# Sixteen feature tiles by seven products, with the weights' block sums made by accumulating transfers

## The chip, the cores and the metric

The kernel runs on one core of a Trainium2 chip. A time is the device's microseconds for one execution. Three runs of the kernel before gave 2389.67, 2389.71 and 2389.91 us, median 2389.71.

## The reference

A decoder trunk of two layers on x of 512 tokens by 1024 features, float32. A layer is a half-step feed-forward, a mixing of three attention branches, and a second half-step feed-forward, each inside RMS norms. The change touches the four feed-forwards alone:

```
D_FF = ((8 * D_MODEL // 3 + 127) // 128) * 128          # 2816 = 22 tiles of 128
def _swiglu(t, w_gate, w_up, w_down):
    return (jax.nn.silu(t @ w_gate) * (t @ w_up)) @ w_down
...
h = h + 0.5 * _rmsnorm(_swiglu(_rmsnorm(h, ffn1_pre_g[l]), ...), ffn1_post_g[l])
```

## The kernel before

**Numbers in two halves.** TensorE multiplies in fp32r. Each operand is split into a high half h (a rounding copy on ScalarE, line 188) and a low half l (source minus h on VectorE, line 189), and a product is three matmuls: h·h, h·l, l·h (`mm3`, lines 214 to 216).

**Weights.** A `Unit` (line 241) is 128x1024 numbers, 512 KB. `fetch` issues its load on SP into one of two "raw" tiles, `load` issues the split into one of four "wh" and one of four "wl" tiles. A `Queue` (line 372) holds the jobs of TensorE in order; when a job starts, the units of the next jobs, four of them, are loaded, so their splits are placed one to two jobs ahead. The order on each engine is fixed when the program is built.

**Feed-forward** (`ffn`, line 642). The 22 feature tiles are made in three ways. Plain jobs (`gates`, `ups`) multiply eight blocks of weights with the tokens for a pair of tiles. Groups of four tiles (`group`, line 766; tiles 2 to 13 in three groups) cut tokens and weights into 2x2 blocks, gate and up side by side, and make the four result blocks with seven products instead of eight (Winograd's form of Strassen's method), tokens on the partitions. The order of the products is `ORDER = (0, 2, 3, 4, 5, 1, 6)`, 24 matmuls of 512 columns each. A group ends with `feature_major` (line 751): 16 transposes and four copies bring its hidden values back to features on the partitions. The first 16 hidden tiles go through the down projection by seven products as well, in two groups of eight tiles (`products`, line 882), the last six plainly (`down`).

**Block sums.** The factors of the seven products are blocks of the weights and sums of them. `BlockUnit` (line 288) loads the blocks from HBM on SP, seven loads for each half of a group, and VectorE makes four sums with `tensor_tensor` on 128x1024 numbers (lines 337, 340, 345, 349) in two kept tiles: kt (tag "v") for gate and up, bt (tag "k") for down. The sums of the tokens (`sums`) and of the hidden values (`first_factor`) are made on VectorE too.

**Order around the change.** In a feed-forward: tile pair 0 (`halved`), pair 14 plainly, groups 2, 6 and 10, then pairs 16, 18 and 20 plainly, their gate and up jobs put between the products of the two down groups. PSUM's eight banks are two tags of four: "mm" for gate and up, "z" for transposes and the down groups. GpSimd (POOL) has little to do: memsets, small copies, two mask selects at the start (lines 144 and 150) and three small loads.

Of the kernel before, what the change touches and what calls it, by code (L numbers as in the profile page):

```python
# [22 lines left out]
def kernel(  # L23
# [84 lines left out]
    def blk(tag, name):  # L108
        return stile([P, 2, S], tag, name)
# [178 lines left out]
    class BlockUnit(Unit):  # L288
# [39 lines left out]
        def load(self):  # L328
# [25 lines left out]
                Q.fetched -= 1  # L354
            Q.fetch_ahead()

    class Keep:


# [274 lines left out]
    W_H, W_U = 4.8, (8.0, 7.0, 7.0, 5.7)  # L634


    TG = (2, 6, 10)

    HR = ("q", "q", "o", "o", "o", "tri", "tri", "rs")
    ORDER = (0, 2, 3, 4, 5, 1, 6)  # L640

    def ffn(l, src, wg, wu, wd, dst, name, spare, aside=None):
# [9 lines left out]
        def hidden(f, pg, pu):  # L652
            s = tmp(f"s{name}_{f}")
            nc.scalar.activation(s[:], pg[:], AF.Silu)
            if f < NC * FC:
                nc.vector.tensor_tensor(pair(f)[:, f % 2], pu[:], s[:], ALU.mult)
                return
            nc.vector.tensor_tensor(s[:], pu[:], s[:], ALU.mult)
            t = blk("q" if f >= 20 else "o", f"hid{name}_{f}")
# [91 lines left out]
        def feature_major(f):  # L751

            for i in range(2):
                u = st.pop(("hid", f, i))
                for b in range(2):
                    f2 = f + 2 * b
                    pt = pbank("z", f"th{name}_{f2}_{i}")
                    for m in range(2):
                        for e in range(2):
                            nc.tensor.transpose(pt[:, (2 * m + e) * P:(2 * m + e + 1) * P],  # L760
                                                u[:, e, (2 * b + m) * P:(2 * b + m + 1) * P], ident[:])
                    yield 0.45
                    out_ = pt[:].rearrange("p (m q) -> p m q", m=2)
                    nc.scalar.copy(pair(f2)[:, :, HALVES[i]], out_)

        def group(f):

            keep = Keep(lambda i, k0: stile([P, 2, S], "v", f"kt{name}_{f}_{i}_{k0}", F32)[:])
            for n in ORDER:
                uns = []  # L770
                for k in range(0, ND // 2, 2):
                    uns.append(BlockUnit(n, wg[l], ND // 2, k, 2, S, keep, f"t{name}_{f}_{n}_{k}", (wg[l], wu[l])))
# [56 lines left out]
        def first_factor(ci, n):  # L829

            nm = f"{name}_{ci}_{n}"
            h, l = (stile([P, FC // 2, S // 2], "v", f"a{x}{nm}")[:] for x in "hl")
            if n == 2:
                st["s", ci] = stile([P, FC // 2, S // 2], "v", f"as{nm}", F32)[:]
            for b in range(2):
                a = lambda i, j: hr[FC // 2 * ci + 2 * j + b][:, :, HALVES[i]]
                two = slice(2 * b, 2 * b + 2)
                s = st["s", ci][:, two] if ("s", ci) in st else None
                if n == 2:
                    nc.vector.tensor_tensor(s, a(1, 0), a(1, 1), ALU.add)  # L840
# [7 lines left out]
                split(h[:, two], l[:, two], from_, scale=-1.0 if n == 6 else None)  # L848
            st["a", ci, n] = h, l


# [30 lines left out]
        def products(ci):  # L882

            def make(i, k0):
                if k0 == 0:
                    st["bt", i] = stile([P, 2, 2, S], "k", f"bt{name}_{i}", F32)
                return st["bt", i][:, k0 // 2]

            keep, w = Keep(make), wd[l, ci * FC * P:(ci + 1) * FC * P]
            for n in ORDER:  # L890
                uns = [BlockUnit(n, w, FC // 2, k, 2, S, keep, f"d{name}_{ci}_{n}_{k}") for k in range(0, FC // 2, 2)]
                yield uns, (lambda n=n, uns=uns: product(ci, n, uns))

        marks, todo = {}, iter(())
# [7 lines left out]
        def some(n):  # L902
            for one in itertools.islice(todo, n):
                Q.add(*one)
# [44 lines left out]
        todo = iter(())  # L949
        pairs = [(wpair(wg[l], ND, f * P, f"g{name}_{f}"), wpair(wu[l], ND, f * P, f"u{name}_{f}")) for f in (16, 18)]  # L950
        Q.add(pairs[0][0], lambda: gates(16, pairs[0][0]))
        behind()
        todo = downs(0)
        Q.add(pairs[0][1], lambda: ups(16, pairs[0][1]))
        some(3)
        Q.add(pairs[1][0], lambda: gates(18, pairs[1][0]))
        some(7)
        Q.add(pairs[1][1], lambda: ups(18, pairs[1][1]))
        todo = downs(1)
        some(3)  # L960
        norm = aside() if aside is not None else None
        xg, xu = wpair(wg[l], ND, 20 * P, f"g{name}_20"), wpair(wu[l], ND, 20 * P, f"u{name}_20")
        Q.add(xg, lambda: gates(20, xg))
        some(4)
        if aside is not None:
            Q.add([], lambda: iter((next(norm),)))
        Q.add(xu, lambda: ups(20, xu))
        if aside is not None:
            Q.add([], lambda: iter((next(norm),)))
        if aside is not None:  # L970
            Q.add([], lambda: norm)
        f0 = NC * FC
        hact = lambda k, c=FULL: tuple(part[:, c] for part in hid[f0 + k])

# [96 lines left out]
    def mem_norm(l, mn):  # L1071
# [1 line left out]
        mn[:] = [stile([P, ND, M], "tri", f"mn{l}_{i}") for i in range(2)]  # L1073
        raws = []
        for t in range(MT):
            raws.append(stile([P, D], "v", f"mraw{l}_{t}", F32))
            nc.sync.dma_start(raws[t][:], mem[0, t * P:(t + 1) * P, :])
        yield 0.0
        for t in range(MT):
# [658 lines left out]
```

## Time and profile before

| | |
|---|---|
| median of 3 runs | 2389.71 us |
| profiled execution | 2390.63 us, its span 2388.9 us |
| granted TensorE clock | 0.999 |
| transfers | 334.00 MB, mean 140 GB/s |
| POOL's own queue (q0) | 96 packets, 0.03 MB |

The names of tiles in the views end with the feed-forward they belong to: a for the first of a layer, c for the second. pta, ptc are PSUM tiles of the gate-up groups, pda, pdc of the down projection, pga and pua of plain gate and up jobs; wh and wl are the halves of weights, tha the transposes of `feature_major`.

### The profile page before, as it was taken

What the parts mean: (1) busy time and instruction counts of PE and PEld (TensorE: products, weight loads), DVE (VectorE), ACT (ScalarE), POOL (GpSimd) and SP (SyncE); (2) the same over time, 40 slices, a digit from 0 to 9 for tenths busy, and PEclk for the clock granted to TensorE, in tenths of its full rate; (3) what the DMA queues carried; (4) which work ended last, traced back from release to release, by engine and by line L of the source; (5) the groups of instructions that cost most, each with busy time, mean ns of one, the idle gap of its engine ahead of it and who ended that gap; (6) DMA issues with size and microseconds to landing.
All of it is one profiled execution on the core that took longest, in us unless ns stands there. A gap on an engine that the chain in (4) does not pass through costs nothing.

```text
span 2388.9 us, 30985 instructions
## 1 busy us (share of the span) xinstructions
PE 2377.2 (100%) x11736; PEld 2010.7 (84%) x11736; DVE 1842.9 (77%) x2535; ACT 1320.8 (55%) x2144; POOL 74.2 (3%) x130
## 2 busy tenths in 40 slices
PE   9999999999999999999999999999999999999998
PEld 8888888888888898888898888888888888988887
DVE  7786887677876687769787878876787766778686
ACT  5655455576655555554545554656675655455543
POOL 0000000001110000000000000000001100000000
PEclk9999999999999999999999999999999999999999
DMA  5554554222223445545545546532232244445453
GB/s 188 165 174 136 202 183 143 71 76 77 88 62 116 158 135 174 169 148 195 184 141 166 178 140 220 174 109 80 63 98 71 71 141 142 159 143 183 141 198 129
DMA packets 233979, 334.00 MB, mean 140 GB/s; under 512 B 10315, under 2 KB 133475, under 8 KB 233829
## 3 DMA queue, kind: packets, MB, share of 16 engines
q1 hardware_dynamic: 233728, 331.98, 42.8%
q8 instruction: 92, 1.51, 0.3%
q14 instruction: 59, 0.48, 0.1%
q0 software_dynamic: 96, 0.03, 0.0%
q10 hardware_dynamic: 4, 0.00, 0.0%
HBM read 319.39 MB, written 12.58 MB: 139 GB/s over the span
## 4 chain that ended last, share of the span: by engine, by line
PE 95%; DVE 3%; ACT 1%; DMA 1%; issue 0%; DVEq 0%; ACTq 0%
PE pg L216 3%; PE pg L214 3%; PE pg L215 3%; PE pta L214 3%; PE ptc L216 3%; PE pta L216 3%; PE ptc L215 3%; PE pta L215 3%; PE ptc L214 3%; PE pda L214 3%; PE pda L215 3%; PE pda L216 3%; PE pdc L216 3%; PE pdc L215 3%; PE pdc L214 3%; PE pb L214 2%
## 5 line engine op out<-in xcount | busy, mean ns | idle before, releaser
L214 PE MATMUL pg<-us_a,wh_wg 128*128 128x512 f32 x384 | 150.6, 392 | 0.0
L216 PE MATMUL pg<-us_a,wl_wg 128*128 128x512 f32 x384 | 149.6, 390 | 0.0
L215 PE MATMUL pg<-us_a,wh_wg 128*128 128x512 f32 x384 | 149.5, 389 | 0.0
L188 ACT CAST wh_tc<-ktc 128x1024 fp32r<-128x1024 f32 x60 | 62.6, 1052 | 83.3 <-DVE ktc L349 32.4
L188 ACT CAST wh_ta<-kta 128x1024 fp32r<-128x1024 f32 x60 | 62.6, 1053 | 80.2 <-DVE kta L349 34.1
L189 DVE TENSOR_TENSOR wl_tc<-ktc,wh_tc 128x1024 fp32r<-128x1024 f32 x60 | 72.8, 1223 | 24.4 <-ACT wh_tc L188 24.2
L189 DVE TENSOR_TENSOR wl_ta<-kta,wh_ta 128x1024 fp32r<-128x1024 f32 x60 | 72.9, 1223 | 23.4 <-ACT wh_ta L188 22.9
L216 PE MATMUL pdc<-wh_dc,alc 128*128 128x512 f32 x224 | 87.3, 390 | 0.3 <-DVE alc L189 0.3
L215 PE MATMUL pdc<-wl_dc,ahc 128*128 128x512 f32 x224 | 87.2, 389 | 0.0
L214 PE MATMUL pdc<-wh_dc,ahc 128*128 128x512 f32 x224 | 87.1, 389 | 0.0
L214 PE MATMUL pda<-wh_da,aha 128*128 128x512 f32 x224 | 87.1, 389 | 0.0
L215 PE MATMUL pda<-wl_da,aha 128*128 128x512 f32 x224 | 87.1, 389 | 0.0
L216 PE MATMUL pda<-wh_da,ala 128*128 128x512 f32 x224 | 87.1, 389 | 0.0
L192 DVE SCALAR_TENSOR_TENSOR wl_wg<-raw_wg,wh_wg 128x1024 fp32r<-128x1024 f32 x48 | 58.8, 1224 | 34.0 <-ACT wh_wg L191 29.5
L216 PEld LDWEIGHTS pg<-us_a,wl_wg 128*128 128x128 f32 x384 | 72.1, 188 | 15.2
L215 PEld LDWEIGHTS pg<-us_a,wh_wg 128*128 128x128 f32 x384 | 72.2, 188 | 14.3
L214 PEld LDWEIGHTS pg<-us_a,wh_wg 128*128 128x128 f32 x384 | 72.1, 188 | 14.3
L214 PE MATMUL pta<-wh_ta,aga 128*128 128x512 f32 x192 | 75.2, 391 | 0.0
L214 PE MATMUL ptc<-wh_tc,agc 128*128 128x512 f32 x192 | 75.0, 391 | 0.0
L216 PE MATMUL pta<-wh_ta,aga 128*128 128x512 f32 x192 | 74.7, 389 | 0.0
L216 PE MATMUL ptc<-wh_tc,agc 128*128 128x512 f32 x192 | 74.7, 389 | 0.0
L215 PE MATMUL ptc<-wl_tc,agc 128*128 128x512 f32 x192 | 74.7, 389 | 0.0
(536 smaller groups left out, 7691.3 us busy)
## 6 DMA issues: line engine op xcount, KB each, us to landing
raw_da<-in_ffn_w_down_dram SPq DMA_DIRECT2D x58, 512.0 KB, 3.6
raw_dc<-in_ffn_w_down_dram SPq DMA_DIRECT2D x58, 512.0 KB, 3.4
raw_ta<-in_ffn_w_gate_dram SPq DMA_DIRECT2D x48, 512.0 KB, 3.7
raw_wg<-in_w_gate_dram SPq DMA_DIRECT2D x48, 512.0 KB, 3.5
raw_tc<-in_ffn_w_gate_dram SPq DMA_DIRECT2D x48, 512.0 KB, 3.6
kta<-in_ffn_w_up_dram SPq DMA_DIRECT2D x24, 512.0 KB, 4.9
raw_wo<-in_w_out_dram SPq DMA_DIRECT2D x24, 512.0 KB, 3.3
ktc<-in_ffn_w_up_dram SPq DMA_DIRECT2D x24, 512.0 KB, 5.7
```

Of the source, the lines that this page charges most:

```text
L188: both = [nc.scalar.copy(h_ap, src)]
L189: make = lambda: nc.vector.tensor_tensor(l_ap, src, h_ap.bitcast(F32), ALU.subtract)
L192: make = lambda: nc.vector.scalar_tensor_tensor(l_ap, src, scale, h_ap.bitcast(F32), ALU.mult, ALU.subtract)
L214: nc.tensor.matmul(pt, lh, rh, start=start, stop=False, skip_group_check=free)
L215: nc.tensor.matmul(pt, lh, rl, start=False, stop=False, skip_group_check=free)
L216: nc.tensor.matmul(pt, ll, rh, start=False, stop=stop, skip_group_check=free)
```

## The change

- The pairs 14 and 16 join as a fourth group (14 to 17), so 16 tiles are made by seven products. Pair 18 takes the place of the early plain pair; only pair 20 stays between the groups, its gate job ahead of the first down group and its up job between the two down groups. Tiles 16 and 17 are split straight from the transposes.
- `SumUnit` replaces `BlockUnit`. VectorE's sums are gone. A tile is negated by ScalarE (`minus`), and a block from HBM, or another tile, is added by a DMA that accumulates, issued by GpSimd (`plus`). Each half of a gate-up group has three kept tiles, six "v" tiles in all, with four accumulating transfers; each half of a down group has two kept tiles with five. Five plain loads are left in each.
- The tiles of mem for `mem_norm` take tag "o" in place of "v", and its parts stand between the products of the second down group.

```
+    class SumUnit(BlockUnit):
+        BLOCKS = ((0, 0), (1, 0), None, None, (1, 1), None, None)
+        def __init__(self, n, src, rows, k0, nk, ncol, keep, name, pair=None, three=True):
+            super().__init__(n, src, rows, k0, nk, ncol, keep, name, pair)
+            self.kept = {2: 0, 3: 2 if three else 1, 5: 1, 6: 0}.get(n)
+            self.three = three
+        def buf(self, i):
+            return self.keep.get(i, self.k0)
+        def plus(self, i, b):
+            if isinstance(b, int):
+                src = self.buf(b)
+            else:
+                r = (b[0] * self.rows + self.k0) * P
+                src, c = (self.src, b[1] * self.ncol) if self.pair is None else (self.pair[b[1]], self.c0)
+                src = src[r:r + self.nk * P, c:c + self.ncol].rearrange("(k p) c -> p k c", p=P)
+            nc.gpsimd.dma_start(self.buf(i), src, accum_op=ALU.add)
+        def minus(self, i, src):
+            nc.scalar.activation(self.buf(i), src, AF.Copy, scale=-1.0)
+        def fetch(self):
...
+            if self.n == 0:
+                self.block(self.buf(1), (0, 1))
+                if self.three:
+                    self.block(self.buf(2), (0, 0))
+        def load(self):
...
+            self.split_from(self.raw[:] if self.kept is None else self.buf(self.kept))
+            if self.n == 0:
+                self.minus(0, self.raw[:])
+                self.plus(0, (0, 1))
+                self.minus(1, self.buf(1))
+                self.plus(1, (1, 1))
+            elif self.n == 2:
+                if self.three:
+                    self.plus(2, 1)
+                else:
+                    self.plus(1, (0, 0))
+            elif self.n == 3:
+                self.minus(0, self.buf(self.kept))
+                self.plus(0, (1, 0))
+                if not self.three:
+                    self.block(self.buf(1), (0, 1))
+            elif self.n == 4 and not self.three:
+                self.minus(1, self.buf(1))
+                self.plus(1, (1, 1))
...
-    HR = ("q", "q", "o", "o", "o", "tri", "tri", "rs")
+    HR = ("q", "q", "o", "o", "o", "o", "o", "tri")
...
-                    nc.scalar.copy(pair(f2)[:, :, HALVES[i]], out_)
+                    if f2 < NC * FC:
+                        nc.scalar.copy(pair(f2)[:, :, HALVES[i]], out_)
+                        continue
+                    if i == 0:
+                        st["hp", f2] = [stile([P, 2, S], "o", f"hid{x}{name}_{f2}") for x in "hl"]
...
+                    split(h[:, :, HALVES[i]], low[:, :, HALVES[i]], out_)
...
-        plain(14, 1, 1)
+        plain(18, 1, 1)
...
-        for g in (6, 10):
+        for g in (6, 10, 14):
...
+        gates_()
         behind()
         todo = downs(0)
...
+        some(7)
+        ups_()
+        todo = downs(1)
+        some(1)
+        norm_()
+        some(3)
+        norm_()
         some(3)
+        norm_(True)
```

More of the change, by code (lines that the diff above doesn't have):

```diff
@@ L847, in first_factor @@
                 from_ = a(*((0, 0), (0, 1), None, None, None, None, (1, 1))[n]) if n in (0, 1, 6) else s
-                split(h[:, two], l[:, two], from_, scale=-1.0 if n == 6 else None)
+                split(h[:, two], l[:, two], from_)
             st["a", ci, n] = h, l
@@ L890, in products @@
             for n in ORDER:
-                uns = [BlockUnit(n, w, FC // 2, k, 2, S, keep, f"d{name}_{ci}_{n}_{k}") for k in range(0, FC // 2, 2)]
+                uns = [SumUnit(n, w, FC // 2, k, 2, S, keep, f"d{name}_{ci}_{n}_{k}", three=False) for k in range(0, FC // 2, 2)]
                 yield uns, (lambda n=n, uns=uns: product(ci, n, uns))
@@ L948, in ffn, with gates_, ups_, norm_ @@
             later[:] = over
-        todo = iter(())
-        pairs = [(wpair(wg[l], ND, f * P, f"g{name}_{f}"), wpair(wu[l], ND, f * P, f"u{name}_{f}")) for f in (16, 18)]
-        Q.add(pairs[0][0], lambda: gates(16, pairs[0][0]))
+        norm = aside() if aside is not None else None
+        xg, xu = wpair(wg[l], ND, 20 * P, f"g{name}_20"), wpair(wu[l], ND, 20 * P, f"u{name}_20")
+        def gates_():
+            Q.add(xg, lambda: gates(20, xg))
+        def ups_():
+            Q.add(xu, lambda: ups(20, xu))
+        def norm_(whole=False):
+            if aside is not None:
+                Q.add([], lambda: norm if whole else iter((next(norm),)))
+        gates_()
         behind()
         todo = downs(0)
-        Q.add(pairs[0][1], lambda: ups(16, pairs[0][1]))
+        some(7)
[3 more added lines that the diff above has]
+        norm_()
         some(3)
[L956 to L959, printed above, removed]
+        norm_()
         some(3)
[L961 to L971, printed above, removed]
+        norm_(True)
         f0 = NC * FC
```

25 lines of the change are left out of this document (21 added, 4 removed).

## The prediction

> **What bounds the kernel now.** I read the page first: its busy shares and the chain that ended last. Then I asked for what TensorE waits for in the whole span.
>
> ```profile
> span 2388.9 us, 30985 instructions
> PE 2377.2 (100%) x11736; PEld 2010.7 (84%) x11736; DVE 1842.9 (77%) x2535; ACT 1320.8 (55%) x2144; POOL 74.2 (3%) x130
> PE 95%; DVE 3%; ACT 1%; DMA 1%; issue 0%; DVEq 0%; ACTq 0%
> PE warm L1608 <- DVE warm L1692: 1.3, 1, 1.3
> PE ptf L1176 <- DVE pf L1247: 0.7, 2, 0.4
> ```
>
> The chain is 95% TensorE, and the waits of TensorE that have a name add up to 4.3 us in seven rows, of which the first two stand here. So nothing but TensorE's own instructions sets the time: an instruction taken off another engine gives nothing back, one taken off TensorE gives its pace, and every new wait of TensorE is paid in full. The pace is not the duration in the groups, since matmuls overlap. It comes from a timeline of TensorE and from the chain in order of time:
>
> ```profile
> 65.72 0.39 PE L214 MATMUL pta<-wh_ta,aga 128*128 128x512 f32 x1
> ...
> 70.93 0.39 PE L216 MATMUL pta<-wh_ta,aga 128*128 128x512 f32 x1
> ```
>
> ```profile
> 109.69 1.75 PE tha L760 x16
> 149.54 1.75 PE tha L760 x16
> ```
>
> The first two rows are matmuls 1 and 24 of one product: 5.21 us for 23 steps, 0.2266 us a matmul of 512 columns. A product (24) takes 5.44 us; a weight unit, half of it, takes u = 2.72 us. Sixteen transposes take 1.75 us. The start to start distance of the two rows, 39.85 us, is a whole group: 7 products (38.1) and one turn (1.75).
>
> **The change, part by part.**
>
> *TensorE.* Four more feature tiles go through seven products in place of eight: 24 fewer matmuls and 16 more transposes per feed-forward, and there are four of these. The instruction orders of the two built programs have it so: 96 fewer 128x512 matmuls, 64 more 128x128 transposes. That is 96 x 0.2266 = 21.8 us less and 4 x 1.75 = 7.0 us more: **-14.8 us**, all on the path.
>
> *VectorE and ScalarE.* 128 sums of 128x1024 leave VectorE, 160 negations of that size come to ScalarE, which is busy 55%. By the reading above both count as nothing, as long as no split comes late. I therefore ask how far ahead the splits run.
>
> ```profile
> L188 ACT CAST wh_da<-bta x40: 1047/1053/1059, 199.2 to 1487.0; 128x1024 fp32r<-128x1024 f32 x40
> L189 DVE TENSOR_TENSOR wl_da<-bta,wh_da x40: 1212/1222/1228, 200.3 to 1488.1; 128x1024 fp32r<-128x1024 f32 x40
> 267.39 1.05 ACT L188 CAST wh_da<-bta 128x1024 fp32r<-128x1024 f32 x1 [1.41 <-PE pda L216]
> 270.11 1.06 ACT L188 CAST wh_ga<-raw_ga 128x1024 fp32r<-128x1024 f32 x1 [1.67 <-PE pda L216]
> 167.18 1.05 ACT L188 CAST wh_ta<-kta 128x1024 fp32r<-128x1024 f32 x1 [3.90 <-DVE kta L349]
> ```
>
> The splits of consecutive units stand 2.72 us apart and wait for TensorE, because there are four buffers of each half: unit i is split when unit i-4 is used up, three units (8.2 us) before it is needed. The split takes 1.05 + 1.22 us, so 5.9 us are in hand. The last row is a split that came 3.9 us late, and TensorE did not feel it.
>
> *The accumulating transfers.* 208 are new: 8 in each gate-up group, 10 in each down group, 512 KB each. They follow a negation on ScalarE and are followed by a split on ScalarE, in ScalarE's fixed order. Let X be the time from the end of the negation to the landing. Nothing in this trace accumulates, so X is bounded by its neighbours: plain transfers, and small ones on the same queue.
>
> ```profile
> raw_wo<-in_w_out_dram SPq DMA_DIRECT2D x24, 512.0 KB, 3.3
> kta<-in_ffn_w_up_dram SPq DMA_DIRECT2D x24, 512.0 KB, 4.9
> bta<-in_ffn_w_down_dram SPq DMA_DIRECT2D x16, 512.0 KB, 5.5
> L123 POOL DMA_DIRECT2D vecs<-in_mem_norm_g_dram x1: 580/580/580, 35.1 to 35.1; - x1
> DMA to landing us min/median/max: 1.8/1.9/2.1
> 100.00:104.00 4.00, 4.00 (x19) 3.33 (x18) 3.96 (x5) 2.01 (x4) 0.00 (x0) 1.00 1.03 369
> 110.00:150.00 40.00, 40.00 (x188) 33.38 (x187) 32.04 (x32) 21.41 (x29) 0.00 (x0) 1.00 0.57 185
> ```
>
> The last two columns of the windows are the share and the GB/s of the 16 transfer engines: full, they move 369 GB/s, so 512 KB (0.524 MB) need 1.4 us of all sixteen; 1.9 us more is what a tiny transfer takes, and the sum, 3.3, is the first row. X cannot be under that 3.3. If the destination must be read too, the work doubles: 1.9 + 2.8 = 4.7. Beside other transfers the plain ones take 1.6 to 2.2 us more (second and third rows); with that X is 6.3 to 6.9. The upper end is three plain passes of 5.5 us one after another, 16.5. I take **X = 7**, nearest to the doubled work in company. Then I look for what each X costs.
>
> 1. *Down products, fourth to fifth factor.* In units from the start of product 0, buffer 1 is free after the split of unit 4 (u + 2.3 = 5.0 us), is loaded again (to 9.5 or so), is negated behind unit 6's split (to 11.1), accumulates, and is split as unit 8, which TensorE needs at 8u = 21.8; less 2.3 for the split, 19.5. So X may be 8.4, and 8.1 for the unit's twin: **8.2**. Beyond it TensorE waits X - 8.2, in 8 places.
> 2. *Gate-up groups.* POOL issues a group's transfers in a fixed order: the sum of buffers 2 and 1 waits there for an earlier landing, and the transfer into buffer 0, which the group's second product needs, is queued behind it. The first negation ends at about 22 us (buffer 1's second half is free after unit 8's split at 5u + 2.3, then 4 us of load and the negation behind unit 10's split), so buffer 0 lands at 22 + 2X + 1 and must land by 16u - 2.3 = 41.2: **X up to 9.1**, beyond it 2(X - 9.1) in 12 places.
> 3. *The start.* In the first feed-forward two mask selects stand on POOL behind an accumulate that waits for another one, and VectorE's copies of the masks stand, in fixed order, ahead of the first weights' low half.
>
> ```profile
> 18.64 2.36 DVE L189 TENSOR_TENSOR wl_ua<-raw_ua,wh_ua 128x1024 fp32r<-128x1024 f32 x2
> 27.80 1.15 POOL L144 TENSOR_SCALAR_AFFINE_SELECT c<-c 128x128 f32<-128x128 f32 x1 [19.73 <-DVE c L143]
> 28.99 0.23 DVE L146 CAST causal<-c 128x128 bf16<-128x128 f32 x1 [0.18 <-POOL c L144]
> 29.27 0.48 DVE L149 MEMSET c<- 128x512 f32 x1
> 31.33 0.43 DVE L152 CAST begins<-c 128x512 bf16<-128x512 f32 x1 [0.50 <-POOL c L150]
> 31.69 1.21 DVE L684 TENSOR_TENSOR ra<-ra,ra 128x1024 f32<-128x1024 f32 x1
> 31.71 0.07 DVE L155 MEMSET c<- 104x8 f32 x1
> 32.82 0.68 DVE L157 TENSOR_SCALAR c<-ident 8x8 f32<-8x8 f32 x4
> 33.53 1.23 DVE L678 TENSOR_TENSOR ra<-us_x 128x1024 f32<-128x1024 f32 x1
> 34.68 0.17 DVE L158 COPY sel<-c 104x8 f32<-104x8 f32 x1
> 34.75 2.35 DVE L189 TENSOR_TENSOR wl_ga<-raw_ga,wh_ga 128x1024 fp32r<-128x1024 f32 x2
> 38.40 0.39 PE L216 MATMUL pga<-us_x,wl_ga 128*128 128x512 f32 x1
> ```
>
>    Buffer 1's load starts when the first low half of the second row's pair (wl_ua) is done, at 19.9; it lands at 24.8 and is negated by 25.9. The first accumulate lands at 25.9 + X = 32.9, POOL issues the next (0.6) and runs the select (1.15): the copy starts at 34.7 and not at 28.99. Behind it stand these steps of VectorE (4.5 us with the copy) and one low half of 1.22 that used to come after wl_ga; then the first half of wl_ga itself (1.22) ends at 41.6 at best, for a matmul that now starts at 38.40: **3.2 us**, once; it grows one for one with X and is gone at X = 3.8.
> 4. *The last turn.* Before, product 0 of the down projection came after an up job of 10.9 us; now it follows the turn of the last group at once, in the same four PSUM banks.
>
> ```profile
> L764 ACT COPY hra<-tha x24: 568/602/628, 111.4 to 1375.9; 128x512 f32<-128x512 f32 x24
> ```
>
>    ScalarE's order puts the split of product 2's second unit (1.05, free only when the gate job ends) and a negation (1.05) ahead of the four copies; the second copied bank needs VectorE's low half as well. From the end of the gate job: 0.6 + 1.05 + 2 x 0.55 + 0.7 = 3.5 us against 1.75 of transposes and 0.68 of matmuls that can go first: **1.05 us, four times, 4.2 us**.
>
> *SP's queue.* It issues 72 fewer loads; the two mem loads now wait for "o" tiles that the first down group has read by then. Nothing; if that group were late, the loads behind them on SP would be as late.
>
> The sum goes against the profiled execution, 2390.6 us (span 2388.9 and 1.7 around it): 2390.6 - 14.8 + 3.2 + 4.2 = 2383.2. The median of the runs is 0.9 lower: **2382.3 us**.
>
> The Trainium skill has a rule against this change. "Collectives: The Full Stack", section "The bandwidth ceiling: the fold count and why AG ≠ RS ≠ AR", says that a reducing transfer runs at half the rate of a copy, since the add needs two source reads, and not because adding is slow. No run here shows it. "DMA: Bandwidth & Descriptors", section "Anatomy of one DMA", gives 2.0 us and 436 GB/s for a transfer of this queue; with two reads X would be 4.4 us by estimate, and the sum 2379.7.
>
> **The rivals.**
>
> - *Late landings* (slower). If issuing such a transfer takes GpSimd several microseconds (the 0.58 above is for eight rows), or company costs more, X passes 8.2. At 8.8 points 1 to 4 eat the whole gain; at 10 the cost is 14 in point 1, 22 in point 2, 6 at the start, 4.5 at the turns: 2421. At 12: about 2490. For it: these chains have no slack to spare. Against it: the estimate from the rows stays under 8.
> - *The transfer engines become the bound* (slower). With doubled work a down group holds 10 x 1.4 + 10 x 2.8 = 42 us of transfers beside 38.1 us of products, a gate-up group 14 + 22.4 = 36.5 beside 39.85. Gate and up jobs between the groups (21.8 us with 5.6 us of transfers) make up for the 4 us. With tripled work it is 56 and 48, which is 18 over (less 8 for those jobs) and 8 over: 8 x 10 + 12 x 8 = 176 us, 2550. This is the rule of the two source reads taken one pass further; with two it does not bind.
> - *The full gain* (faster). If X is under 5 or the start and the turns find cover, 2375 to 2380.
> - *It doesn't do what it says*: the work taken off VectorE is worth nothing here, since VectorE ends no wait of TensorE above 0.7 us. That is in the sum already; only the 14.8 us count.
>
> **How the numbers follow.** My forecast (X from 5.5 to 8.3, 2380 to 2385) has 0.37, the full gain 0.12, X between, where gain and cost cancel, 0.11, late landings 0.32, full transfer engines 0.08. A measurement can tell about 0.2% (4.8 us) from no change, so faster is under 2384.9: 0.48; slower over 2394.5: 0.40; within: 0.12. The range goes down to the full gain less a little, 2374, and up to X = 10.5, 2440, which leaves out the far end of late landings and the full engines. The likeliest case's own range is 2379 to 2386.
>
> **What would show it.** TensorE: 96 and 64 in the counts, groups still 39.85 us apart. The landing of the POOL transfers into kta and bta: 6 to 8 us. In TensorE's waits: wl_ga once, about 3 us; pda for a copy or low half after the turn, about 1 us four times; none for wh_ta or wh_da. I would be wrong if landings were above 8.2 us: then wh_da (fifth factor) and wh_ta (second product) appear among TensorE's waits 8 and 12 times; or if the share of the transfer engines were near 1 through whole groups.

## The result, and the profile after

The changed kernel takes **2567.8 us** (median of 4 runs, 2564.4 to 2570.8) against 2389.7 before: 1.0746 times as long, interval 1.0732 to 1.0759. It is slower by 178 us, where 7 us less was forecast. The profiled execution took 2564.4 us; its span is 2562.7 us, 173.8 longer than before.

The page of the changed kernel, in the order busy time, queues, chain:

```profile
PE 2434.1 (95%) x11704; PEld 2026.9 (79%) x11704; DVE 1695.0 (66%) x2415; ACT 1503.2 (59%) x2358; POOL 313.2 (12%) x338
q0 software_dynamic: 52576, 109.09, 25.1%
PE 54%; DMA 23%; DVE 8%; ACT 7%; issue 7%; POOL 1%; ACTq 0%; POOLq 0%; SPq 0%; DVEq 0%
```

The chain was 95% TensorE; now 23% of it are transfers. TensorE sits idle for 128.6 us (11.7 before), and though it has 14.8 us less to do it is busy for 57 us more. Two losses, then: waits, and slower matmuls. The waits of TensorE (line waited for, us in total, times, longest):

```profile
PE ptc L214 <- ACT cc L810: 23.4, 11, 3.7
PE pta L214 <- ACT ca L810: 22.5, 11, 4.0
PE pda L214 <- ACT hra L836: 8.8, 2, 4.4
PE pda L214 <- ACT aha L188: 7.9, 2, 4.4
...
PE vecs_t L128 <- DMA vecs<-in_b_gate_dram: 4.1, 1, 4.1
PE pda L215 <- DVE wl_da L189: 3.7, 6, 0.8
...
PE pga L216 <- DVE wl_ga L189: 1.0, 1, 1.0
```

The large ones are not for weights. Line 810 is ScalarE's Silu of the seventh product, which empties two PSUM banks (an evacuation); line 836 copies the transposes, which empties four; aha and ahc are factors made of hidden values. Landings of the transfers (the last column, us):

```profile
bta<-in_ffn_w_down_dram POOLq DMA_DIRECT2D x40, 512.0 KB, 8.1
kta<-in_ffn_w_up_dram POOLq DMA_DIRECT2D x32, 512.0 KB, 8.2
```

The turns (the 16 transposes) of the four groups of the first feed-forward, from timelines of TensorE, with the first matmul of the first group and the last down matmul:

```profile
66.08 0.80 PE L214 MATMUL pta<-wh_ta,us_x 128*128 128x512 f32 x1
...
127.76 1.91 PE L831 MATMUL tha<-ident,ca 128*128 128x128 f32 x16
...
175.45 1.91 PE L831 MATMUL tha<-ident,ca 128*128 128x128 f32 x16
...
222.67 1.91 PE L831 MATMUL tha<-ident,ca 128*128 128x128 f32 x16
...
262.51 1.91 PE L831 MATMUL tha<-ident,ca 128*128 128x128 f32 x16
...
409.73 0.39 PE L216 MATMUL pda<-wh_da,hida 128*128 128x512 f32 x1
```

They are 47.69, 47.22 and 39.84 us apart: a group costs nothing extra when no group follows it. Such rows cut every run into stages, summed over the four feed-forwards below: the gate-up stage from the first matmul of the groups to the last turn, the down stage from there to the last down matmul. "Counted" is the kernel before with the 14.8 us off: each gate-up stage 128.6 us plus a group of 39.85, the down stages the rest. The stage columns come from each run's profiled execution, the last column is the run's time.

| kernel | gate-up stages | down stages | whole, us |
|---|---|---|---|
| counted for the new order | 674 | 491 | 2376 |
| the changed kernel | 761 | 585 | 2567.8 |
| VectorE's sums (e1) | 675 | 517 | 2408.0 |
| transfers for gate and up only (e3) | 760 | 516 | 2501.3 |
| transfers for down only (e4) | 687 | 594 | 2491.1 |
| plain transfers (e5) | 676 | 512 | 2401.4 |
| evacuation first (e6) | 738 | 597 | 2553.0 |
| and POOL's order (e12) | 702 | 598 | 2515.9 |

Of e3 to e7, e10 and e12 there is one time each, of the others a median. The changed kernel's profiled execution is 189 us above the count of its own order. Of these, 87 are lost in the gate-up stages, all but some 3 of them in twelve places, three in each feed-forward; 94 are lost in the down stages, 5.9 at the start and 1.7 elsewhere.

**One of the twelve places, on three engines.** TensorE first, at the second product of the second group (start, duration, and in brackets the idle time before it with what ended it):

```profile
117.18 0.50 PE L214 MATMUL pta<-wh_ta,aga 128*128 128x512 f32 x1 [3.96 <-ACT ca L810]
...
120.67 0.80 PE L214 MATMUL pta<-wh_ta,aga 128*128 128x512 f32 x1 [1.95 <-ACT ca L810]
121.26 0.63 PE L215 MATMUL pta<-wl_ta,aga 128*128 128x512 f32 x1
...
125.10 0.51 PE L215 MATMUL pta<-wl_ta,aga 128*128 128x512 f32 x1
```

ScalarE, in its fixed order, shortly before:

```profile
115.59 1.04 ACT L188 CAST wh_ta<-kta 128x1024 fp32r<-128x1024 f32 x1 [6.06 <-DMA kta<-in_ffn_w_up_dram]
116.54 0.59 ACT L810 ACTIVATE ca<-pta 128x512 f32<-128x512 f32 x1
119.07 1.04 ACT L188 CAST wh_ta<-kta 128x1024 fp32r<-128x1024 f32 x1 [1.94 <-DMA kta<-in_ffn_w_up_dram]
120.02 0.59 ACT L810 ACTIVATE ca<-pta 128x512 f32<-128x512 f32 x1
```

Each Silu needs 0.59 us. Its input was ready at about 108, when the last matmul of the seventh product was through, but it stands behind a split that waits for a landing. And GpSimd, which issued those transfers:

```profile
91.96 1.20 POOL L382 DMA_DIRECT2D kta<-in_ffn_w_up_dram  x1 [21.49 <-ACT kta L385]
95.02 1.20 POOL L382 DMA_DIRECT2D kta<-in_ffn_w_up_dram  x1 [1.85 <-ACT kta L385]
99.88 0.90 POOL L382 DMA_DIRECT2D kta<-kta  x1 [3.66 <-DMA kta<-in_ffn_w_up_dram]
105.06 0.86 POOL L382 DMA_DIRECT2D kta<-kta  x1 [4.28 <-DVE wl_ta L189]
105.61 2.79 POOL L382 DMA_DIRECT2D kta<-in_ffn_w_up_dram  x2
```

The first transfer, issued at 91.96, has landed by 99.88. The last two go into buffer 0; they could not be issued before the two sums of tiles, and are used at 115.59 and 119.07, 10 and 12 us later. The transfer engines are full while these wait (the last two columns are their share and GB/s):

```profile
96.00:116.00 20.00, 17.22 (x76) 13.92 (x75) 9.25 (x10) 8.32 (x9) 4.46 (x5) 1.00 1.05 233
```

The second loss is in the granted clock (the column behind POOL's busy time):

```profile
112.00:116.00 4.00, 1.22 (x6) 0.68 (x4) 0.00 (x0) 0.41 (x1) 0.00 (x0) 1.00 1.10 239
116.00:120.00 4.00, 1.27 (x3) 0.48 (x3) 1.23 (x1) 2.06 (x3) 0.00 (x0) 0.81 0.61 132
120.00:124.00 4.00, 3.33 (x8) 2.69 (x9) 2.89 (x3) 4.00 (x7) 2.14 (x2) 0.50 0.08 6
```

After the wait the clock is granted at half, and from 121.26 to 125.10 nine matmuls take 0.427 us each instead of 0.2266: 1.8 us on top of the wait. In the whole timeline 180 steps from one matmul of a product to the next are 0.39 to 0.46 us long, none before; they alone are some 36 us more than at full pace.

### The profile page after: what moved, and what is told of

It reads as the page before. It is cut to its first block, busy times and chain, and to the rows that moved or that the text cites. A ratio compares the mean times of both kernels' runs of the same rounds, so it can differ in the third digit from the quotient of the medians.

```text
span 2562.7 us, 31463 instructions
## 1 busy us (share of the span) xinstructions
PE 2434.1 (95%) x11704; PEld 2026.9 (79%) x11704; DVE 1695.0 (66%) x2415; ACT 1503.2 (59%) x2358; POOL 313.2 (12%) x338
## 3 DMA queue, kind: packets, MB, share of 16 engines
q0 software_dynamic: 52576, 109.09, 25.1%
## 4 chain that ended last, share of the span: by engine, by line
PE 54%; DMA 23%; DVE 8%; ACT 7%; issue 7%; POOL 1%; ACTq 0%; POOLq 0%; SPq 0%; DVEq 0%
DMA ktc<-in_ffn_w_up_dram 7%; DMA kta<-in_ffn_w_up_dram 5%; DMA bta<-in_ffn_w_down_dram 4%; PE pg L216 3%; PE pg L214 3%; PE pg L215 3%; DMA btc<-in_ffn_w_down_dram 3%; DVE wl_tc L189 1%; PE pb L214 1%; PE pb L216 1%; PE pb L215 1%; PE pda L215 1%; PE pda L214 1%; PE pda L216 1%; PE pq L214 1%
## 5 line engine op out<-in xcount | busy, mean ns | idle before, releaser
L189 DVE TENSOR_TENSOR wl_ta<-kta,wh_ta 128x1024 fp32r<-128x1024 f32 x64 | 78.3, 1224 | 109.7 <-ACT wh_ta L188 109.6
L189 DVE TENSOR_TENSOR wl_tc<-ktc,wh_tc 128x1024 fp32r<-128x1024 f32 x64 | 78.3, 1223 | 108.4 <-ACT wh_tc L188 108.4
L214 PE MATMUL pta<-wh_ta,aga 128*128 128x512 f32 x256 | 107.5, 420 | 23.3 <-ACT ca L810 22.5
L214 PE MATMUL ptc<-wh_tc,agc 128*128 128x512 f32 x256 | 106.3, 415 | 23.4 <-ACT cc L810 23.4
L215 PE MATMUL pta<-wl_ta,aga 128*128 128x512 f32 x256 | 105.4, 412 | 1.6 <-DVE wl_ta L189 1.6
L214 PE MATMUL pdc<-wh_dc,ahc 128*128 128x512 f32 x224 | 92.6, 414 | 15.0 <-ACT hrc L836 7.0
L215 PE MATMUL ptc<-wl_tc,agc 128*128 128x512 f32 x256 | 105.1, 411 | 1.3 <-DVE wl_tc L189 1.3
L216 PE MATMUL pta<-wh_ta,aga 128*128 128x512 f32 x256 | 104.6, 408 | 0.0
L216 PE MATMUL ptc<-wh_tc,agc 128*128 128x512 f32 x256 | 104.1, 407 | 0.0
L189 DVE TENSOR_TENSOR wl_tc<-raw_tc,wh_tc 128x1024 fp32r<-128x1024 f32 x48 | 58.4, 1223 | 60.4 <-ACT wh_tc L188 60.4
L189 DVE TENSOR_TENSOR wl_ta<-raw_ta,wh_ta 128x1024 fp32r<-128x1024 f32 x48 | 58.6, 1224 | 58.0 <-ACT wh_ta L188 57.8
L382 POOL DMA_DIRECT2D ktc<-in_ffn_w_up_dram x32 | 40.4, 1299 | 389.2 <-ACT nhb L582 280.9
```

What stands on the lines that cost most here:

```text
L189: make = lambda: nc.vector.tensor_tensor(l_ap, src, h_ap.bitcast(F32), ALU.subtract)
L214: nc.tensor.matmul(pt, lh, rh, start=start, stop=False, skip_group_check=free)
L215: nc.tensor.matmul(pt, lh, rl, start=False, stop=False, skip_group_check=free)
L216: nc.tensor.matmul(pt, ll, rh, start=False, stop=stop, skip_group_check=free)
L382: nc.gpsimd.dma_start(self.buf(i), src, accum_op=ALU.add)
```

## The experiments

The theory after reading the trace: the accumulating transfers land late, and what TensorE then misses is mostly not the weights but work queued behind a waiting split on ScalarE. The rivals: full transfer engines, the new order of the jobs, GpSimd's issue.

**e1, VectorE's sums in the new order.**

```
-uns.append(SumUnit(n, wg[l], ...))    +uns.append(BlockUnit(n, wg[l], ...))
-uns = [SumUnit(n, w, ...)]            +uns = [BlockUnit(n, w, ...)]
-split(h[:, two], l[:, two], from_)    +split(h[:, two], l[:, two], from_, scale=-1.0 if n == 6 else None)
```

> The changed kernel's four groups and order of jobs, with the block sums back on VectorE (no accumulating transfer). Theory (the accumulating transfers and what stands behind them in fixed orders cost everything): the 14.8 us of TensorE come out, less at most the 1 us at each of the four last turns: 2375 to 2380 us. Rival (the new order itself costs: the down groups back to back, the last turn ahead of them): the 96 us that the down stages lost in the changed kernel stay at least in part, 2420 us or more.

Measured 2408.0 us, 1.0073 times before (1.0059 to 1.0086). Both expectations missed, and it is the main surprise: without a single accumulating transfer the sixteen tiles make the kernel slower. The gate-up stages take what was counted to a microsecond; the down stages lose 26 us, and most of the rest is lost right behind them, where TensorE waits for the norm (utc and uta, 4.7 us in all). VectorE's windows in the first down stage (third busy figure), and what TensorE waits for:

```profile
231.00:271.00 40.00, 40.00 (x178) 32.84 (x176) 38.04 (x46) 24.56 (x35) 0.00 (x0) 1.00 0.41 134
271.00:311.00 40.00, 37.22 (x155) 29.53 (x155) 37.73 (x46) 20.40 (x27) 0.00 (x0) 0.96 0.56 193
```

```profile
PE pda L214 <- ACT aha L188: 5.6, 5, 2.2
```

VectorE is busy 95% (88% before, in its windows from 230 to 310, when gate and up jobs stood between these products), and the factors of hidden values come late.

**e2, the transfers in the old order.** SumUnit in the kernel before, nothing else.

> The kernel before, with its three groups and its jobs between the products of the down groups; only the block sums are made by negation and accumulating transfers. Theory (late landings): two places of some 7 us in each of four feed-forwards, 57 us, and some 10 us in the down stages of each, which the gate and up jobs between cover in part: 2470 to 2500 us. Rival (full transfer engines: 40.7 us of their time in a gate-up group of 39.85, but room in the down stages, where 132 us stand against 141): under 2450 us. Rival (the new order of jobs costs): 2390 to 2400 us.

Measured 2483.0 us, 1.0392 (1.0378 to 1.0406), as the theory had it. The gate-up stages lose 63 us, nearly all of it in eight such places. So the transfers cost 92 us without the new order, and the rival of full engines, which had under 2450, is weakened.

**e3 and e4, the transfers in one stage only.** SumUnit kept for gate and up (e3) or for down (e4), BlockUnit in the other.

> The changed kernel, with the sums of the down groups back on VectorE; accumulating transfers in the gate-up groups alone. Theory (each stage pays for its own transfers): 2567.8 less the 96 us that the down stages lost, 2465 to 2480 us, with the three places per feed-forward at a group's second product unchanged at some 7 us each. Rival (the new order of jobs costs in the down stages): above 2500 us.

> The changed kernel, with the sums of the gate-up groups back on VectorE; accumulating transfers in the down groups alone. Theory: 2567.8 less the 85 us of the gate-up groups and some 5 us at the start, 2470 to 2485 us. Rival (the gate-up groups are late for another reason, such as ScalarE's negations or POOL): above 2520 us.

Measured 2501.3 and 2491.1 us. Each stage pays for its own transfers (table); both are above their ranges. e3 reaches its rival's (above 2500), by what e1 loses in the down stages too. e4 is over by 12 us at the end of the gate-up stages, when the first accumulating transfers of the down groups are under way (issued from 196 us in the first feed-forward); that these hold up the last gate-up blocks was not tested. Against e1 the transfers cost 93 us in gate and up and 83 in down.

**e5, plain transfers.**

```
-nc.gpsimd.dma_start(self.buf(i), src, accum_op=ALU.add)
+nc.gpsimd.dma_start(self.buf(i), src)
```

> The changed kernel with every accumulating transfer as a plain one: same queue, same orders, same bytes, nothing is added, so the sums are left out. Theory (the price is the add in the transfer): landings fall from 8.2 to some 5 us, below the 8.2 and 9.1 us that the chains allow, and the time falls to 2380 to 2410 us. Rival (GpSimd's issue of 1.2 us and the fixed orders of POOL and ScalarE are enough by themselves): above 2480 us.

Measured 2401.4 us: the add is the price, not GpSimd's issue or the orders by themselves. (By e8 a plain transfer also takes GpSimd 0.5 us less to issue; this run does not separate that.) The same bytes on the same queue, and their landing:

```profile
q0 software_dynamic: 30048, 109.09, 13.3%
kta<-in_ffn_w_up_dram POOLq DMA_DIRECT2D x32, 512.0 KB, 5.1
```

13.3% of 2399.7 us is 319 us of the sixteen engines; with the add it was 25.1% of 2562.7, 643 us, 2.0 times as much.

**e6, the evacuation first.** The splits of the next group's second product are placed behind the seventh product's two Silus.

```
+if i > self.at + 1 and getattr(un, "pair", None) is not None and un.n == 2:
+    self.hold = False; return               # in load_ahead
-nc.scalar.activation(t[:, e], pts[e][:], AF.Silu)
+tc.keep_in_program_order(nc.scalar.activation(t[:, e], pts[e][:], AF.Silu))
+Q.pinned = self.n == 2 and self.three       # around split_from
```

> The changed kernel, with ScalarE's two evacuations of the seventh product put ahead of the splits for the next group's second product, in all twelve places. Theory A (TensorE waits for PSUM banks whose evacuation stands behind late splits, and the landing itself is in time): the 85 us of the gate-up groups go to under 20, 2490 to 2505 us. Theory B (the landing itself is late by some 4 us, and the order on ScalarE adds the rest): about half of it stays, 2520 to 2540 us, and TensorE then waits for wh_ta and not for line 810's tile. Rival (full transfer engines): no change, 2555 to 2570 us.

Measured 2553.0 us. That is 13 us above theory B's range and just under the rival's. The gate-up stages gain 23 us of the 87 and the down stages lose 11 of them again; TensorE now waits for wh_ta, as theory B said:

```profile
PE pta L214 <- ACT wh_ta L188: 13.7, 5, 4.4
```

Theory A falls: the queue behind the split is about a quarter of it, the late landing itself the rest.

**e7, the sum of two tiles on VectorE.**

```
-self.plus(2, 1)
+nc.vector.tensor_tensor(self.buf(2), self.buf(2), self.buf(1), ALU.add)
```

> The changed kernel, with one of the four sums of a gate-up group's half, that of two tiles in SBUF, made by VectorE; the transfer that stood ahead of the one into buffer 0 on POOL is gone, and with it 2 of 8 accumulating transfers of a group. Theory (POOL's fixed order makes the landing late): the transfer into buffer 0 is issued as soon as its negation is done, 3 to 5 us sooner, and most of the 85 us go, 2485 to 2510 us. Rival (full transfer engines, 40.7 us a group): demand falls to some 35 us, the groups come back to 39.85 us, 2480 us, and the landings fall under 7 us. Rival (the length of one transfer decides alone): under 25 us gained.

Measured 2589.9 us, 22 slower than the changed kernel, against all three expectations.

```profile
kta<-in_ffn_w_up_dram POOLq DMA_DIRECT2D x32, 512.0 KB, 6.0
DVE kta L412 <- DMA kta<-in_ffn_w_up_dram: 55.5, 14, 5.2
PE ptc L214 <- DVE cc L814: 20.6, 6, 4.5
```

The landings did fall, from 8.2 to 6.0, and yet the time rose: now VectorE waits for a landing, and its PSUM evacuations (line 814) stand behind that. The transfer engines' share from turn to turn fell as well, from 0.89 and 0.87 to 0.75, and the groups still take 49.4 and 47.1 us, so full engines are not the bound over a whole group here. That they have no part in the late landings is not shown: in the changed kernel they are full for the 20 us ahead of one (the window above).

**e12, POOL's order.** e6, and the transfers into buffer 0 are issued ahead of the sums of tiles.

```
+with tc.issue_after(self.keep.first.ins):   # first: the transfer into buffer 0
+    add()
```

> The run with the evacuation first, with one thing more: on POOL the transfers into buffer 0 stand ahead of the two sums of tiles, which wait there for an earlier landing. Theory (buffer 0 is late because its issue waits some 3 us behind these, and two then run together): the second product's units land 2 to 4 us sooner, the gate-up stages lose 5 us less each time, 2490 to 2520 us against 2553. Rival (the length and the company of the transfers alone): within 10 us of 2553. Rival (the sum of tiles, now behind, is late for the third product): no gain, and TensorE waits there instead.

Measured 2515.9 us, 37 less than e6, and all of it in the gate-up stages (738 to 702). For the second group of the first feed-forward the two are issued at 102.66 and 105.95 and used at 109.82 and 113.29, 7 us later and no longer 10 and 12. Taken in this sequence, ScalarE's order is 23 of the 87 us and POOL's 37; the 28 that are left, put down to the length and company of the transfers, were not tested further.

**e8, the prices alone.** A kernel that copies x to the output and holds nothing else but the transfers and matmuls to be priced.

> The disputed costs by themselves; the kernel copies x to the output and leaves the trunk out. Transfers of 512 KB on POOL's queue: plain, accumulating from HBM, accumulating from SBUF, each alone, then six in a row, then six accumulating beside six plain ones of SP. Then runs of 100 matmuls behind pauses of growing length. Theory (the add itself is dear): alone an accumulating one lands 6 to 8 us after its issue, a plain one after 3.5 to 4.5; six in a row land 3 us apart or more, against 1.5 for plain ones. Rival (company is dear, the add is not): alone under 5 us, and it is the mixture that brings 8. Pauses: under 1 us the matmuls keep their pace of 0.227 us but for the first; after 3.5 us or more some ten of them take 0.43 us.

GpSimd's rows; a COPY reads what has just landed:

```profile
48.13 0.72 POOL L89 DMA_DIRECT2D one<-in_w_in_dram  x1 [0.28 <-issue]
52.41 0.18 POOL L75 COPY flag<-one 128x8 f32<-128x8 f32 x1 [3.56 <-DMA one<-in_w_in_dram]
52.88 1.23 POOL L92 DMA_DIRECT2D add<-in_w_in_dram  x1 [0.28 <-issue]
59.02 0.18 POOL L75 COPY flag<-add 128x8 f32<-128x8 f32 x1 [4.91 <-DMA add<-in_w_in_dram]
...
108.86 0.19 POOL L75 COPY flag<-sums 128x8 f32<-128x8 f32 x1 [1.28 <-DMA sums<-in_w_in_dram]
111.39 0.19 POOL L75 COPY flag<-sums 128x8 f32<-128x8 f32 x1 [2.34 <-DMA sums<-in_w_in_dram]
114.95 0.19 POOL L75 COPY flag<-sums 128x8 f32<-128x8 f32 x1 [3.37 <-DMA sums<-in_w_in_dram]
118.99 0.19 POOL L75 COPY flag<-sums 128x8 f32<-128x8 f32 x1 [3.85 <-DMA sums<-in_w_in_dram]
```

Alone, a plain transfer is usable 4.3 us after its issue and an accumulating one after 6.1. In a row the accumulating ones follow 2.5 us apart, plain ones 1.3, with the engines' share at 1.09 and 0.90. SP's plain transfers started earlier than meant, at 108, so the second half of this row shows the mixture: 3.6 and 4.0 us apart, about the sum of the two. So both hold: the add doubles the work, and company on full engines brings the rest. TensorE's rows, with the pause in brackets:

```profile
179.84 22.96 PE L122 MATMUL gp<-wsb,gap 128*128 128x512 f32 x100 [1.51 <-DVE gap L129]
204.77 24.59 PE L122 MATMUL gp<-wsb,gap 128*128 128x512 f32 x100 [1.97 <-DVE gap L129]
```

With one pause of each length: those of 1.0 and 1.5 us cost only themselves; behind those of 2.0, 2.4, 3.4, 4.7 and 7.0 us the hundred matmuls take 1.5 to 2.2 us more.

**e9, e10, e11: what e1 lost.** e9 puts the 16 down sums of a feed-forward on GpSimd, e10 leaves them out, e11 is e9's edit in the kernel before.

```
-nc.vector.tensor_tensor(t, t, self.raw[:], ALU.subtract)
+(nc.vector if self.pair else nc.gpsimd).tensor_tensor(t, t, self.raw[:], ALU.subtract)   # e9, e11; all four sums
+if self.pair is not None: ...                                                             # e10
```

> The new order of jobs with no accumulating transfer, as in the run with VectorE's sums, but the 16 sums of the two down groups of each feed-forward stand on GpSimd, which has nothing else to do there. Theory (in the back-to-back down groups VectorE is the bound: 38.04 us busy of 40, and TensorE waits for factors that it splits late): the 32 us between 2408 and the forecast's 2376 come back, 2376 to 2384 us, faster than the kernel before. Rival A (the new order of jobs costs in another way, by the last turn and the PSUM banks): still 2400 us or more. Rival B (GpSimd's sums are slow, over 2.7 us each, or disturb VectorE at the memory): above 2400 us, with waits of TensorE for wh_da.

> The same with the block sums of the down groups left out: blocks are split as they are loaded, so these products are not the reference's. Theory (VectorE is the bound there): the lower end of what relief can give, 2374 to 2379 us. Rival (the order costs in another way): 2400 us or more.

> The kernel before, in its own order, with the sums of the down groups on GpSimd. The prediction held that taking sums off VectorE is worth nothing there, since gate and up jobs between the products give it time (35.3 us of 40): 2388 to 2392 us. Rival (VectorE held it back unseen): under 2385 us. If GpSimd's sums are too slow: above 2395 us.

Measured 2453.3 (1.0269, 1.0250 to 1.0288), 2389.3 and 2404.7 us (1.0060, 1.0043 to 1.0077). e10: VectorE's sums are 19 of the 32 us, by one run. Of the 13 that are left, 4.5 are two waits of TensorE for the banks of the mem transposes, which used to stand behind an up job. e9 and e11 are rival B, and the reason is in two rows:

```profile
248.90 2.72 POOL L345 TENSOR_TENSOR bta<-bta,raw_da 128x1024 f32<-128x1024 f32 x1 [2.42 <-issue]
```

```profile
249.29 3.41 DVE L189 TENSOR_TENSOR wl_da<-bta,wh_da 128x1024 fp32r<-128x1024 f32 x1
```

A VectorE instruction of 1.22 us, begun while GpSimd's sum runs, ends 1.1 us after it, here and in all 29 such cases of this run. GpSimd's help costs VectorE the time of the help: with 64 sums less it is busy for 1912 us, against 1915 in e1. The Trainium skill ("SBUF — State Buffer", section "Who interferes with whom") says just this: a VectorE instruction with two SBUF inputs and a GpSimd one that reads SBUF need the same read port, and one blocks until the other is through; the rows agree. For this reason e11 does not tell what VectorE's relief alone is worth in the old order; that stays open.

**e13a, e13d, e13g: the place of the up job.** e1, with the one up job of the down stage moved from between the down groups to behind the fourth product of the second (a), behind the fourth of the first (d), or behind the second group (g).

```
-some(7); ups_(); todo = downs(1); some(1); norm_(); some(3); norm_(); some(3); norm_(True)
+some(7); todo = downs(1); some(1); norm_(); some(3); ups_(); norm_(); some(3); norm_(True)     # a
+some(4); ups_(); some(3); todo = downs(1); some(1); norm_(); some(3); norm_(); some(3); norm_(True)   # d
+some(7); todo = downs(1); some(1); norm_(); some(3); norm_(); some(3); ups_(); norm_(True)     # g
```

> Four groups with VectorE's sums; only the up job moves, from between the two down groups to behind the fourth product of the second. Eleven products then follow one another without a break. Theory of total work: 2403 to 2413 us, as before the move (2408). Theory of place: the long row makes VectorE later, 2415 us or more, or, if the break is better placed late, under 2400.

> The same, with the up job moved behind the fourth product of the first down group; ten products follow without a break. Theory of total work: 2403 to 2413 us. Theory of place: over 2415 us, since the backlog of VectorE falls into the second group.

> The same, with the up job moved behind the second down group, ahead of the mem transposes. Fourteen products follow without a break. Theory of total work: 2403 to 2413 us, less some 4 us where the job covers what follows. Theory of place: over 2420 us from VectorE's backlog, or under 2395 if the end of the stage (mem transposes, norm) is what costs.

Measured 2400.5 (1.0045, 1.0030 to 1.0060), 2420.8 (1.0129, 1.0114 to 1.0144) and 2418.8 us (1.0119, 1.0104 to 1.0135). None lies in the 2403 to 2413 of total work: place matters, by 20 us.

**e15, one sum by a transfer.** e1, with only the seventh product's down sum accumulated.

```
+if self.n == 3:
+    nc.scalar.activation(t, t, AF.Copy, scale=-1.0)
+    nc.gpsimd.dma_start(t, <block (1, 0)>, accum_op=ALU.add)    # used three products later
```

> Four groups with VectorE's sums, but of the four sums of a down group's half the last (seventh product) is made by a negation and an accumulating transfer, which has three products, 16 us, to land. VectorE has 16 sums of 1.22 us less in all, 4.9 us in each down stage; two raw loads per group go too. Theory of total work on VectorE: about half of the 19 us that leaving out all sums gave, 2396 to 2402 us, and no wait for the landing, since 16 us are more than the 8 to 12 it takes. Rival (an accumulating transfer costs wherever it stands, by ScalarE's fixed order): above 2408 us.

Measured 2395.4 us (1.0018, 1.0009 to 1.0028), 13 under e1: less work on VectorE counts too, and an accumulating transfer with three products to land costs nothing to be seen (it lands in 5.9 us).

**e16 and e17, both together.** e15 with the up job behind the fourth product of the second down group (e16), or the third (e17).

```
+some(1); norm_(); some(2); ups_(); some(1); norm_(); some(3); norm_(True)    # e17
```

> The last down sum by an accumulating transfer, and the up job behind the fourth product of the second down group. Two causes that add: 2408 less 13 less 8, 2386 to 2389 us, a little faster than the kernel before. One cause: 2392 to 2397 us.

> The same, with the up job behind the third product. If place still matters, over 3 us from the other run, to either side; if VectorE now has room, the same within 2 us.

Measured 2396.2 (1.0027, 1.0017 to 1.0037) and **2385.1 us (0.9983, 0.9974 to 0.9992)**. They do not simply add, and one product of difference is worth 11 us. e17 is faster than both kernels, by 0.17% of the one before: of the 14.8 us, 4.5 can be had. One of its windows:

```profile
270.00:310.00 40.00, 39.55 (x173) 32.09 (x172) 39.26 (x49) 23.97 (x30) 2.37 (x2) 1.00 0.64 191
```

VectorE is at least as full as in e1, but TensorE is idle 0.45 us in place of 2.78. A full VectorE thus costs only where something urgent stands behind its backlog. The difference between e16 and e17 is such a place. In e16 TensorE waits there in every feed-forward (pdc for ahc the same, 4.2, 2, 2.1); e17 has no such wait:

```profile
PE pda L214 <- ACT aha L188: 4.4, 2, 2.2
```

In the first feed-forward ScalarE casts this factor at nearly the same time in both, at 282.92 and 282.33. In e16 the third product of the second group wants it at 281.4 and starts at 283.60; in e17, as the order was built, ten matmuls of the up job stand ahead of that product, from 280.62 to 283.26, and cover the delay. These waits, 8.6 us in four feed-forwards, are nearly all of the 8.7 us by which the spans of the two profiled executions differ.

## Why the prediction was wrong

The step that failed is the price of the new waits. The sum held X = 7 to be under the limits of points 1 and 2 and added nothing for them, and it gave the four last turns 4.2 us. In their place stand 87 us in the gate-up stages and 94 in the down stages, because the transfers were used 8 to 12 us after their issue and because more was queued behind each late split than its own product. Part by part:

- **TensorE's part, -14.8 us: right.** The counts came as said, an undisturbed turn to turn is 39.84 us, and e1's gate-up stages take 675 us where 674 were counted.
- **VectorE's relief, to "count as nothing, as long as no split comes late": failed.** It was read from a stage in which gate and up jobs stood between the down products. The change takes most of them out and nothing was reckoned for that: e1 loses 32 us, of which VectorE's sums are 19 (e10). The change itself pays for this with the transfers, so in its own 178 us the term is hidden; it is why undoing the transfers does not bring the gain.
- **X = 7: near for one alone, short in company.** Alone 6.1 from issue to use, in the kernel 8 for the first transfer of a group and 10 and 12 for those into buffer 0. The doubled work was right (319 and 643 us of the engines).
- **Point 1 (fifth down factor): right in the first down group, wrong in the second.** In the first no wait of TensorE there is over 0.6 us. In the second the negation ends at 339.6 and the split follows at 348.74, so X was 9.1 and over the limit of 8.2. TensorE pays in the fourth product, for a factor that is queued behind that split on ScalarE; it does so in all four feed-forwards, 13.0 us in all (aha and ahc). The pieces of up to 1.0 us for wh_da and wl_da are mostly at the second group's second and third products.

```profile
348.74 1.04 ACT L188 CAST wh_da<-bta 128x1024 fp32r<-128x1024 f32 x1 [3.53 <-DMA bta<-in_ffn_w_down_dram]
350.36 0.60 PE L214 MATMUL pda<-wh_da,aha 128*128 128x512 f32 x1 [3.50 <-ACT aha L188]
```

- **Point 2 (buffer 0 behind POOL's order): mechanism right, size wrong.** It had the first negation end at 22 us of the group and buffer 0 land at 22 + 14 + 1 = 37, with 41.2 the limit. The transfers were issued at 25.9 and 28.9 (91.96 and 95.02 less the group's start, 66.08), the second half sets the pace, and buffer 0 was used at 49.5 and 53. e12 confirms the order on POOL: 37 us.
- **The step that was missing:** each wait was priced by what the late weights themselves hold up. Behind a split that waits, ScalarE's order holds two PSUM evacuations in each of the twelve places (23 us by e6), and in the down stages the copies of the last turn and the factors of the second group. Point 4 saw one such place and gave it 1.05 us; idle there were 3.4 to 4.5 us each time.
- **The clock: not reckoned.** That "every new wait of TensorE is paid in full" was too little: by e8, one of 2 us or more is paid with 1.5 to 2.2 us on top. Of the 71.7 us by which TensorE's busy time is above 2377.2 - 14.8, the 180 slow steps are some 36; another 31 or so are first matmuls behind idle time, which the profile counts at their full 0.4 to 0.8 us and not at the pace. The Trainium skill ("TensorE: Matmul & The Clock Gate", section "What's actually happening") has half the clock after an idle window of some 3.4 us, and full speed after as long a busy one; the halving and the length of the slow stretch agree (granted 0.50; behind the 2.0 us pause of e8 some eight steps of 0.427 us), but here pauses of 2.0 us were enough.
- **The start: 5.9 us for 3.2.** The wait for wl_ga is 1.0; 4.1 go to the loads of vecs, which stand on POOL behind the first accumulating transfers. The mask selects were seen, these were not.
- **The rivals.** Late landings was the case, but its prices (2421 at X = 10, 2490 at 12) lacked the queue behind the splits, the clock and most of the down stages' 94 us, of which e5 shows 73 to be the add's price; the other 21 are left without the add. Full transfer engines as a bound on whole groups was not (e7), but its demand was put too low: the first two stretches from turn to turn hold 42 and 41 us of the engines' time (0.89 of 47.69 and 0.87 of 47.22), where 36.5 was reckoned beside 39.85 of products. By itself that would be 1 to 3 us of the 7 to 8 lost in each, and e8 shows what such sharing does to a landing. That the relief of VectorE is worth nothing is refuted for the new order by e10 and e15.

How the 73 us of the down stages divide was not tested apart. TensorE's idle time names three places: 15.9 us at the turns (hra, hrc), some 18 at the second and third products of the second group, 13.0 behind the split of its fifth factor (aha, ahc). The slow clock behind these waits comes on top.

## What to carry to other kernels

A new wait on an in-order engine costs what it waits for and what is queued behind it: of the 87 us of the gate-up stages, ScalarE's queue was 23 and POOL's 37. So list the next instructions there, PSUM evacuations first. A transfer that adds in memory took twice the engines' time here and belongs where several products lie between its issue and its use, as in e15 and e17. And read the slack of an engine in the order of work that the change leaves, not in the one that it found.

## What the hardware showed that was not expected

- An accumulating transfer of 512 KB takes 6.1 us alone against 4.3, GpSimd issues it in 1.2 us against 0.7, and it needs 2.0 times the transfer engines' time.
- A pause of TensorE of 1.5 us left the clock alone, one of 2.0 us halved it for a while.
- A GpSimd sum in SBUF stretched a VectorE subtraction begun beside it from 1.22 to 3.41 us.
- Accumulating transfers in a row fill the transfer engines (share 1.09) at one 512 KB transfer in 2.5 us.
